# Scale and shift of the MLP's LayerNorm input: from whole rows on GpSimd ahead of the transposes to columns on ScalarE behind them

## The chip, the core and the metric

The kernel runs on one core of a Trainium2 chip. The metric is the device time of one execution in microseconds (us); of several runs the median is taken. The kernel before took 2519.69 us in the median of three runs (2519.55 to 2523.37).

A core has a matrix engine (PE, TensorE), whose weight loads the profile lists apart (PEld), and three engines that work on 128 partitions at a time: VectorE (DVE), ScalarE (ACT) and GpSimd (POOL). SyncE (SP) issues the loads and most stores. They work side by side, each in its own program order, and wait for one another by semaphores. Operands lie in SBUF; PE writes its products to PSUM, which DVE and ACT read.

## The reference, cut to what matters

One inference step of one decoder layer for a prompt of 2048 tokens and 32 sample tokens, in fp32, of width 1024:

```python
mixed = jnp.einsum('bte,ed->btd', jnp.concatenate([y_ssm, y_att], -1), w_out)
x = layer_norm(ALPHA * x + g_m * mixed, ln1_g, ln1_b)
h = x * (1.0 + sc_f) + sh_f
u = jnp.square(jax.nn.relu(jnp.einsum('btd,df->btf', h, w_up)))
f = jnp.einsum('btf,fd->btd', u, w_down)
x = layer_norm(ALPHA * x + g_f * f, ln2_g, ln2_b)
```

`sc_f`, `sh_f`, `g_m` and `g_f` are rows of 1024 numbers, computed from the sequence's vector `c`; for the prompt there is one of each, the same for all its tokens. The LayerNorm's own gain and shift (`ln1_g`, `ln1_b`) and the two rows behind it fold into one scale and one shift for each of the 1024 columns: with the normalised row u, h = u A2 + B2, where A2 = ln1_g (1 + sc_f) and B2 = ln1_b (1 + sc_f) + sh_f.

## The kernel before

The program has three large stages: the input projection with the mixers (to about 790 us of the span), the **output projection** with LayerNorm 1 (790 to 1009 us), and the **MLP** (to the end). The change lies in the second.

**Precision.** Each fp32 matmul operand is split into a high and a low part (`split`, L160: a rounding copy by ScalarE is the high part at L161, source minus high part is the low part at L162, by DVE unless another engine is named). A product is then three matmuls (`mm3`, L165 to L167): high times high, high times low, low times high.

**The output projection** runs over sixteen tiles of 128 tokens. The steps of a tile t are functions:

- `out_a(t)` (L1037) loads the tile's two halves of the mixers' output into one staging buffer, transposes one of them on PE (four transposes, L1047), and splits both. The low part of the loaded half is POOL's for tiles 1 to 3 and DVE's otherwise.
- `out_x(t)` (L1054) loads the tile's residual and scales it by two DVE operations over 128x1024 (L1057, L1058), which read and write SBUF alone.
- `out_mm(t)` (L1062) is the projection, 2 x 8 x 3 = 48 matmuls of 128x512.
- `out_u(t)` (L1073) multiplies the result out of PSUM by the gate row (L1079), adds the residual (L1080), takes the statistics (L1081, L1082, L172; the power -1/2 on POOL, L173), forms one column `nbo` on DVE (L1085), and normalises on ScalarE (L1086) with that column and `rs` as bias and scale. The result u is stored (L1087), as the second LayerNorm's residual.
- `out_h(t)` (L1090) is h = u A2 + B2, two operations over 128x1024 on POOL (L1095, L1096), on DVE in the last tile. A2 and B2 are rows that `out_rows` (L1029) has spread over all 128 partitions: four broadcast loads of 512 KB and three DVE operations. h has a single buffer, `ho`.
- `out_c(t)` (L1107) transposes h on PE, two sets of four 128x128 (L1118), and splits each set out of PSUM: ScalarE copies 128x512 to the high part, DVE subtracts for the low part. Tiles 0 to 7 land in `H2`, which stays in SBUF for the MLP's first half; there a tile's 1024 numbers lie in eight strips of 128 with gaps. Tiles 8 to 15 go to `h2_d` in DRAM.

The code calls them as `out_mm(t)`, `out_u(t)`, `out_h(t)`, `out_c(t - 1)`. The order on each engine is not the code's order: a scheduler in the compiler sorts the instructions of all engines by a model of their times, so that PE's transposes of one tile stand among the matmuls of a later one.

**The MLP** starts with `up`, which squares the up-projection by DVE (L1261) and takes a low part by POOL (L1262), with weights that are loaded, scaled by a row `gf` on DVE (L1137) and split by ScalarE and POOL; and with `acc_init`, which turns eight tiles of stored u into the second residual by two DVE operations each (L1231, L1232). The buffers of `A2`, `B2`, `ho`, `x1` and `u1` serve the MLP as well.

Of the kernel before, what the change touches and what calls it, by code (L numbers as in the profile page):

```python
# [23 lines left out]
NTILE = T // 128  # L24
# [47 lines left out]
def host_arrays(i):  # L72
    a = {}
    f = lambda n: np.asarray(i[n])
    a["consts"], a["dmask"] = host_consts()
    a["x"] = np.concatenate([f("x_prompt")[0], f("x_sample").reshape(ND, DM)], 0)
    c = np.concatenate([f("c_prompt"), f("c_sample")], 0)
    a["cT"] = c.T.reshape(8, 128, 9).transpose(1, 0, 2)
    wa = f("w_ada")[0].reshape(8, 128, 6144)
    wc = wa[:, :, :2048].reshape(2, 4, 128, 2, 8, 128)[:, :, :, ::-1].transpose(4, 0, 2, 1, 3, 5)  # L80
    a["w_ac"] = wc.reshape(8, 2, 128, 1024)
    a["w_ada"] = wa[:, :, 2048:].reshape(8, 128, 8, 512).transpose(2, 1, 0, 3)
    col = lambda v: v.reshape(-1, 128).T
# [14 lines left out]
    a["normw"] = f("ssm_norm_w")
    a["rows"] = np.stack([f("ln_in_g"), f("ln_in_b"), f("ln1_g")[0], f("ln1_b")[0], f("ln2_g")[0], f("ln2_b")[0]], 0)
    wo = f("w_out")[0]  # L100
    att = wo[512:].reshape(2, 4, 64, 1024)[:, HR].transpose(1, 0, 2, 3).reshape(4, 128, 1024)
    a["wo"] = np.concatenate([wo[:512].reshape(4, 128, 1024), att], 0)
    a["wu"] = f("w_up")[0].reshape(8, 128, 32, 128).transpose(2, 1, 0, 3)
    a["wd"] = f("w_down")[0].reshape(32, 128, 1024)
    a["h0"] = f("state_ssm")[0].reshape(8, 512, 128).transpose(0, 2, 1)
    ck, cv = f("cache_k")[0], f("cache_v")[0]
    a["ckT"] = ck.transpose(3, 2, 0, 1).reshape(64, 2, 1024)
    a["ck"] = ck.reshape(8, 128, 128)
    a["cv"] = cv.reshape(8, 128, 128)
    return {k: np.ascontiguousarray(v) for k, v in a.items()}  # L110
# [8 lines left out]
def body(tc, I, O):  # L119
    nc = tc.nc  # L120
    V, S, G, PE, D = nc.vector, nc.scalar, nc.gpsimd, nc.tensor, nc.sync
# [3 lines left out]
    def pool(name, **kw):  # L125
        return tc.alloc_tile_pool(name=name, bufs=1, reuse_waits="tile", **kw)
# [9 lines left out]
    def sc_tile():  # L136
        return ps.tile([128, 512], F32, tag="sc", name="sc", bufs=3)
# [3 lines left out]
    ada_d = tc.dram_tile([9, 6 * DM], F32, name="ada_d")  # L141
# [18 lines left out]
    def split(hi, lo, src, eng=None):  # L160
        S.activation(hi, src, AF.Copy)  # L161
        (eng or V).tensor_tensor(lo, src, hi.bitcast(F32), ALU.subtract)  # L162
# [19 lines left out]
    def bcast(t, src):  # L182
        D.dma_start(out=t, in_=src.partition_broadcast(t.shape[0]))
        return t
# [11 lines left out]
    ident = idt[:, 0:128]  # L196
# [431 lines left out]
    blk = {}  # L628
# [56 lines left out]
    n = len(seq)  # L685
# [66 lines left out]
    for i in range(n + 3):  # L752
# [3 lines left out]
        t = g(i)  # L756
# [216 lines left out]
    def prt(i, dt_=F32):  # L973
        return pr.tile([128, 1024], dt_, tag=f"p{i}", name=f"p{i}")
# [19 lines left out]
    first2 = {}  # L994

    def q2(nm, dt_=F32):
        return first2.pop(nm) if nm in first2 else pr2.tile([128, 1024], dt_, tag=nm, name=nm)
# [11 lines left out]
    def o_y():  # L1009
        i = ocnt["y"]  # L1010
        ocnt["y"] += 1
        if i < 2:
            r = hb2[i][:, 0], hb2[i][:, 1]
        elif i == 2 or i > 3 and i % 3 == 0:
            r = prt(5, F32R), prt(6, F32R)
        else:
            r = [p3.tile([128, 1024], F32R, tag="y" + c, name="y" + c, bufs=2) for c in "hl"]
        return [t.rearrange("p (k n) -> p k n", k=8) for t in r]

    ag, ab_ = prt(2), prt(3)  # L1020
    orow = {}

    def ada_row(r, j, P):
        if P == 128:
            return bcast(r, ada_d[0, 1024 * j:1024 * j + 1024])
        D.dma_start(out=r[:ND], in_=ada_d[1:9, 1024 * j:1024 * j + 1024].unsqueeze(1).to_broadcast([NB, NT_, 1024]))
        return r

    def out_rows(P):  # L1029
        A2, B2 = [ada_row(t, j, P) for t, j in ((q2("A2"), 4), (q2("B2"), 3))]  # L1030
        g1 = bcast(q2("ho"), I["rows"][2])
        b1 = bcast(p3.tile([128, 1024], F32, tag="yh", name="b1", bufs=2), I["rows"][3])
        V.scalar_tensor_tensor(b1[:P], A2[:P], 1.0, b1[:P], ALU.add, ALU.mult)
        V.tensor_tensor(B2[:P], B2[:P], b1[:P], ALU.add)
        V.scalar_tensor_tensor(A2[:P], A2[:P], 1.0, g1[:P], ALU.add, ALU.mult)
        return A2, B2

    def out_a(t):
        P = ptok(t)
# [14 lines left out]
    def out_x(t):  # L1054
        x = o_x(t)
        D.dma_start(out=x, in_=I["x"][128 * t:128 * t + 128])
        V.scalar_tensor_tensor(x, x, mean_all[:, t, 0:1], ag, ALU.subtract, ALU.mult)  # L1057
        V.scalar_tensor_tensor(x, x, mean_all[:, t, 1:2], ab_, ALU.mult, ALU.add)  # L1058
        blk["ox", t] = x

    def out_mm(t):
        yh, yl = blk.pop(("o", t))  # L1062
        blk["om", t] = mms = []
        for n in range(2):
            sl = slice(512 * n, 512 * n + 512)
            mm = sc_tile() if t == 1 else mm_tile()
            for k in range(8):
                mm3(mm, yh[:, k, :], yl[:, k, :], Wo[k][0][:, sl], Wo[k][1][:, sl], k == 0, k == 7)
            mms.append(mm)
# [17 lines left out]
        D.dma_start(out=xhat1_d[128 * t:128 * t + 128], in_=u)  # L1087
        blk["ou", t] = u

    def out_h(t):  # L1090
        A2, B2 = orow[0]
        u = blk.pop(("ou", t))
        h = q2("ho")
        eng = V if t == NTILE - 1 else G
        eng.tensor_tensor(h, u, A2, ALU.mult)  # L1095
        eng.tensor_tensor(h, h, B2, ALU.add)  # L1096
        blk["h2", t] = h

    def out_b_dec():
        yh, yl = blk.pop(("o", NTILE))  # L1100
        ud = o_x(1)
        for n in range(2):
            sl = slice(512 * n, 512 * n + 512)
            mm_dec(ud[:, sl], 512, lambda k: yh[:, k, :2 * ND], lambda k, l: Wo[k][l][:, sl])
        S.dma_start(out=ud_d, in_=ud[:2 * ND])

    def out_c(t):  # L1107
        h = blk.pop(("h2", t))
        if t < 8:
            sl = slice(128 * (t % 4), 128 * (t % 4) + 128)  # L1110
            oh, ol = H2[t // 4][0][:, :, sl], H2[t // 4][1][:, :, sl]
        else:
            oh, ol = o_y()
        for j in range(2):
            tr = sc_tile().rearrange("p (k n) -> p k n", k=4)
            for kk in range(4):
                k = 4 * j + kk
                PE.transpose(tr[:, kk, :], h[:, 128 * k:128 * k + 128], ident)  # L1118
            split(oh[:, 4 * j:4 * j + 4, :], ol[:, 4 * j:4 * j + 4, :], tr)
        if t >= 8:  # L1120
            D.dma_start(out=h2_d[t - 8][:, 0], in_=oh.bitcast(F32))
            D.dma_start(out=h2_d[t - 8][:, 1], in_=ol.bitcast(F32))
# [18 lines left out]
    def wu_pq():  # L1141
        return [pq.tile([128, 1024], F32R, tag="wu" + c, name="wu" + c) for c in "hl"]
# [16 lines left out]
    pk.release()  # L1159
    cs_.release()  # L1160
    pr2 = pool("pr2", side="right")
    first2.update({nm: pr2.tile([128, 1024], F32, tag=nm, name=nm) for nm in ("x1", "u1", "A2", "B2", "ho")})
    pq = pool("wu", side="right")
    ph = pool("h2", side="right")
    H2 = [[ph.tile([128, 8, 512], F32R, name=f"H2_{j}{i}") for i in range(2)] for j in range(2)]
    p3 = pool("out")
    out_a(2)
    out_x(2)
    out_a(3)
    out_x(1)  # L1170
    orow[0] = out_rows(128)
    for t in range(NTILE):
        if t > 2:
            out_a(t + 1)
        if 1 < t < NTILE - 1:
            out_x(t + 1)
        if t > 1:
            out_mm(t)
        if t > 0:
            out_u(t)  # L1180
        out_h(t)
        if t > 0:
# [209 lines left out]
    for half in range(2):  # L1392
# [24 lines left out]
        for fb in range(15):  # L1417
            f = 2 * fb
# [19 lines left out]
        for j in range(3):  # L1438
            for i in range(2):
                a = 352 * j  # L1440
                while a < 352 * (j + 1):
                    e = min((a // 128 + 1) * 128, 352 * (j + 1))
                    D.dma_start(out=H3[j][i][:, :, a - 352 * j:e - 352 * j].bitcast(F32),
                                in_=h2_d[a // 128][:, i, :, a % 128:a % 128 + e - a])
                    a = e
# [78 lines left out]
```

## Time and profile before

| | |
|---|---|
| median of 3 runs | 2519.69 us (2519.55 to 2523.37) |
| the profiled execution | 2522.31 us |
| its span, first to last instruction | 2520.5 us |
| granted TensorE clock, mean | 0.985 |
| busy: PE / DVE / POOL / ACT | 96 / 60 / 37 / 29 % of the span |
| slices 14 to 16 of 40 (63 us each, 819 to 1008 us), busy in tenths: PE | 9, 8, 8 |
| the same: DVE / POOL / ACT | 9, 8, 8 / 5, 4, 4 / 2, 2, 2 |

How to read what follows. Times are us from the start of the span, unless marked ns. A row of a timeline has the start, the duration, the engine, the line of the program, the operation, what it writes and reads, and the shape (partitions x elements); "x4" means four instructions in a row, and the bracket at the end tells how long the engine stood idle ahead of it and what ended that. A row of groups has the count, the busy time in all, the mean of one in ns, and the idle time ahead of the group's instructions with what ended it. A row of waits reads "engine, what it was to write, its line <- engine, what that wrote, its line: us in total, times, the longest". L161, L162 and L165 to L167 are helpers' lines; there the names tell which step it is: `yh` and `yl` (or `p`) are the high and low parts of the mixers' output, `H` and some `yh`, `yl` those of h, `mm` the projection's result, `sc` and `tr` PSUM of the transposes, `pg` the projection's weights. Buffer numbers are left out there.

### The profile page before, as it was taken

To read this page: it belongs to the slowest core of one execution; us is meant where nothing else is said; L and a number is where in the kernel's file an instruction comes from. 1 tells how busy PE (TensorE), PEld (TensorE's weight loads), DVE (VectorE), ACT (ScalarE), POOL (GpSimd) and SP (SyncE) were. 2 spreads that over 40 slices of the span, in tenths; PEclk is the share of its full clock that TensorE was granted. 3 is DMA by queue.
4 is the path that set the end of the run, shared out by engine and by line. 5 is a ranking of instruction groups with operands and counts; after the bars stand their busy time and mean duration, and the time that the engine had idled before them with its cause. 6 is when DMAs were issued, how large, how long until landed. Compare 5 with 4: busy or idle time off the path is not lost.

```text
span 2520.5 us, 32205 instructions
## 1 busy us (share of the span) xinstructions
PE 2421.1 (96%) x12694; PEld 2004.7 (80%) x12694; DVE 1510.5 (60%) x2582; ACT 720.2 (29%) x1434; POOL 930.8 (37%) x602
## 2 busy tenths in 40 slices
PE   7899999999998988899999999999999999999997
PEld 6567787977997766787888888887788988988985
DVE  6756666977788988744434444447844344344347
ACT  3544465333342222222121211213221221221221
POOL 4323431233223544633243333426532332332335
PEclk9999999999999999899999999999999999999998
DMA  8644333223335336411111211118211111111111
GB/s 318 255 173 160 118 124 91 73 72 109 98 115 174 117 127 221 162 59 58 48 59 42 63 51 39 53 43 238 100 51 34 43 59 34 43 59 34 43 46 70
DMA packets 116504, 244.19 MB, mean 97 GB/s; under 512 B 25984, under 2 KB 61248, under 8 KB 113200
## 3 DMA queue, kind: packets, MB, share of 16 engines
q1 hardware_dynamic: 111952, 232.15, 27.6%
q10 hardware_dynamic: 4400, 9.98, 1.1%
q8 instruction: 100, 1.64, 0.3%
q14 instruction: 52, 0.43, 0.1%
HBM read 187.74 MB, written 55.37 MB: 96 GB/s over the span
## 4 chain that ended last, share of the span: by engine, by line
PE 53%; DVE 3%; POOL 1%; issue 1%; DMA 0%; ACT 0%; SPq 0%; POOLq 0%; DVEq 0%; ACTq 0%
PE sc L165 10%; PE sc L167 10%; PE sc L166 10%; PE mm L165 5%; PE mm L167 5%; PE mm L166 5%; PE tr L165 2%; PE tr L167 2%; PE tr L166 2%; PE tr L1276 1%; DVE p L1231 1%; DVE nb L1300 0%; DVE p L1232 0%; POOL rs L173 0%; DVE p L1307 0%
## 5 line engine op out<-in xcount | busy, mean ns | idle before, releaser
L162 POOL TENSOR_TENSOR wdl<-st,wdh 128x1024 fp32r<-128x1024 f32 x63 | 164.1, 2605 | 531.4 <-ACT wdh L161 531.4
L1261 DVE TENSOR_TENSOR r<-r 128x320 f32<-128x320 f32 (+1 forms) x160 | 151.3, 946 | 299.0 <-ACT u L1257 101.6
L1288 DVE TENSOR_TENSOR p<-mm,p 128x512 f32<-128x512 f32 x298 | 202.7, 687 | 176.6 <-PE mm L167 176.6
L161 ACT ACTIVATE wdh<-st 128x1024 fp32r<-128x1024 f32 x63 | 66.8, 1061 | 628.4 <-PE mm L167 245.4
L165 PE MATMUL sc<-H,wvh 128*128 128x352 f32 (+1 forms) x640 | 227.1, 355 | 5.3 <-ACT r L1255 5.3
L167 PE MATMUL sc<-H,wvl 128*128 128x352 f32 (+1 forms) x640 | 226.1, 353 | 0.0
L166 PE MATMUL sc<-H,wvh 128*128 128x352 f32 (+1 forms) x640 | 225.9, 353 | 0.0
L165 PE MATMUL sc<-H,wuh 128*128 128x352 f32 (+1 forms) x640 | 224.4, 351 | 0.0
L167 PE MATMUL sc<-H,wul 128*128 128x352 f32 (+1 forms) x640 | 223.9, 350 | 0.0
L166 PE MATMUL sc<-H,wuh 128*128 128x352 f32 (+1 forms) x640 | 223.6, 349 | 0.0
L1255 ACT ACTIVATE r<-sc 128x352 f32<-128x352 f32 (+1 forms) x160 | 81.7, 511 | 271.6 <-PE sc L167 230.9
L165 PEld LDWEIGHTS sc<-H,wvh 128*128 128x128 f32 x640 | 120.8, 189 | 18.3 <-ACT r L1255 5.7
L166 PEld LDWEIGHTS sc<-H,wvh 128*128 128x128 f32 x640 | 120.7, 189 | 12.0
L167 PEld LDWEIGHTS sc<-H,wvl 128*128 128x128 f32 x640 | 120.4, 188 | 12.1
L165 PEld LDWEIGHTS sc<-H,wuh 128*128 128x128 f32 x640 | 120.4, 188 | 11.4 <-ACT r L1255 0.8
L167 PEld LDWEIGHTS sc<-H,wul 128*128 128x128 f32 x640 | 120.8, 189 | 10.5
L166 PEld LDWEIGHTS sc<-H,wuh 128*128 128x128 f32 x640 | 120.7, 189 | 10.2
L1137 DVE TENSOR_TENSOR st<-st,gf 128x1024 f32<-128x1024 f32 x64 | 83.8, 1309 | 55.6 <-POOL wdl L162 46.3
L1288 DVE TENSOR_TENSOR p<-tr,p 128x512 f32<-128x512 f32 x102 | 69.9, 687 | 74.8 <-PE tr L167 74.8
L173 POOL TENSOR_TENSOR rs<-ve,mhalf 128x1 f32<-128x1 f32 (+2 forms) x68 | 49.1, 722 | 174.9 <-DVE ve L172 158.1
L1260 DVE TENSOR_TENSOR ud<-r 128x32 f32<-128x32 f32 x32 | 56.5, 1766 | 94.4 <-ACT r L1255 94.4
L652 DVE SCALAR_TENSOR_TENSOR xc<-xq,cvw,xc 128x256 f32<-128x256 f32 x192 | 102.0, 535 | 2.7
(485 smaller groups left out, 6630.8 us busy)
## 6 DMA issues: line engine op xcount, KB each, us to landing
st<-in_wd SPq DMA_DIRECT2D x64, 512.0 KB
st<-in_wu SPq DMA_DIRECT2D x63, 512.0 KB
wa<-in_w_ada SPq DMA_DIRECT2D x32, 512.0 KB
hT_d<-hb SPq DMA_DIRECT2D x16, 1024.0 KB
hT<-hT_d SPq DMA_DIRECT2D x16, 512.0 KB
hT<-hT_d SPq DMA_DIRECT2D x8, 1024.0 KB
csb<-cs_d SPq DMA_DIRECT2D x16, 512.0 KB
p<-xhat_d SPq DMA_DIRECT2D x16, 512.0 KB
```

Of the source, the lines that this page charges most:

```text
L161: S.activation(hi, src, AF.Copy)
L162: (eng or V).tensor_tensor(lo, src, hi.bitcast(F32), ALU.subtract)
L165: PE.matmul(out, lhsT=ahi, rhs=bhi, start=first, stop=False)
L166: PE.matmul(out, lhsT=ahi, rhs=blo, start=False, stop=False)
L167: PE.matmul(out, lhsT=alo, rhs=bhi, start=False, stop=last)
L173: G.tensor_tensor(r[:P], v[:P], mhalf[:P, 0:n], ALU.pow)
L652: V.scalar_tensor_tensor(dst_, src(j), cvw[:, f, j:j + 1], dst_, ALU.mult, ALU.add)
L1137: V.tensor_tensor(st, raw, scale, ALU.mult)
L1255: S.activation(r[:, :n], mm[:, :n], AF.Relu)
L1260: V.tensor_tensor(ud, r[:, w:n], r[:, w:n], ALU.mult)
L1261: V.tensor_tensor(r[:, :w], r[:, :w], r[:, :w], ALU.mult)
L1288: V.tensor_tensor(acc[t][:, sl], mm, acc[t][:, sl], ALU.add)
```

## The change

The scale and shift move behind the transpose. In a transposed tile the 1024 columns lie on the partitions, eight groups of 128, so A2 and B2 become columns: one number per partition and group, sixteen columns in all (`AB2`).

- `out_rows` and its rows go; `out_cols` takes their place: the two rows from DRAM are loaded as a 16x128 block and turned by one PE transpose, the two LayerNorm rows come from the host as 128x16 (`lcol`), and three small DVE operations form `AB2`. Buffers `A2` and `B2` are no longer taken in this stage.
- `out_h` goes. `out_c` transposes u itself.
- Behind the transposes ScalarE makes eight passes of 128x128, each with one column of A2 as scale and one of B2 as bias, out of PSUM into `ho`.
- The whole h is split at once: ScalarE's copy of 128x1024, and the subtraction of 128x1024 on POOL (on DVE in the last tile), where there were two copies out of PSUM and two subtractions on DVE.

```diff
+    a["lcol"] = np.concatenate([col(f("ln1_g")[0]), col(f("ln1_b")[0])], 1)
...
-    def out_rows(P):
-        A2, B2 = [ada_row(t, j, P) for t, j in ((q2("A2"), 4), (q2("B2"), 3))]
-        g1 = bcast(q2("ho"), I["rows"][2])
-        b1 = bcast(p3.tile([128, 1024], F32, tag="yh", name="b1", bufs=2), I["rows"][3])
-        V.scalar_tensor_tensor(b1[:P], A2[:P], 1.0, b1[:P], ALU.add, ALU.mult)
-        V.tensor_tensor(B2[:P], B2[:P], b1[:P], ALU.add)
-        V.scalar_tensor_tensor(A2[:P], A2[:P], 1.0, g1[:P], ALU.add, ALU.mult)
-        return A2, B2
+    def out_cols():
+        AB2 = pr2.tile([128, 2, 8], F32, name="AB2")
+        t_ = p3.tile([128, 1024], F32, tag="yh", name="lc", bufs=2)
+        r16 = t_[:16, 0:128]
+        D.dma_start(out=r16, in_=ada_d[0, 3072:5120].rearrange("(k p) -> k p", p=128))
+        lc = t_[:, 128:144].rearrange("p (a k) -> p a k", a=2)
+        D.dma_start(out=lc.rearrange("p a k -> p (a k)"), in_=I["lcol"])
+        tr = sc_tile()
+        PE.transpose(tr[:, 0:16], r16, ident[:16, :16])
+        for i in range(2):
+            V.scalar_tensor_tensor(AB2[:, i], tr[:, 8:16], 1.0, lc[:, i], ALU.add, ALU.mult)
+        V.tensor_tensor(AB2[:, 1], AB2[:, 1], tr[:, 0:8], ALU.add)
+        return AB2
...
-    def out_h(t):
-        A2, B2 = orow[0]
-        u = blk.pop(("ou", t))
-        h = q2("ho")
-        eng = V if t == NTILE - 1 else G
-        eng.tensor_tensor(h, u, A2, ALU.mult)
-        eng.tensor_tensor(h, h, B2, ALU.add)
-        blk["h2", t] = h
...
     def out_c(t):
-        h = blk.pop(("h2", t))
+        u = blk.pop(("ou", t))
...
+        h = q2("ho").rearrange("p (k n) -> p k n", k=8)
         for j in range(2):
             tr = sc_tile().rearrange("p (k n) -> p k n", k=4)
             for kk in range(4):
                 k = 4 * j + kk
-                PE.transpose(tr[:, kk, :], h[:, 128 * k:128 * k + 128], ident)
-            split(oh[:, 4 * j:4 * j + 4, :], ol[:, 4 * j:4 * j + 4, :], tr)
+                PE.transpose(tr[:, kk, :], u[:, 128 * k:128 * k + 128], ident)
+            for kk in range(4):
+                k = 4 * j + kk
+                S.activation(h[:, k, :], tr[:, kk, :], AF.Identity, bias=AB2[:, 1, k:k + 1], scale=AB2[:, 0, k:k + 1])
+        split(oh, ol, h, V if t == NTILE - 1 else G)
```

The lines of the changed kernel are one to five higher: L1052 has the transposes of `out_a`, L1062 and L1063 the residual, L1084 to L1091 `out_u`, L1115 the transposes of u, L1118 the eight passes, L162 and L163 the split, L166 to L168 `mm3`.

The scheduler orders the changed program anew. On PE, the place is where the transposes of a middle tile stand. Before, those of tile 2's h (`ho_8410`) were in the midst of the 48 matmuls of tile 5 (`mm_8676`):

```order
L167 MATMUL mm_8676<-pg8_8027,yl_8534 128x512
L165 MATMUL mm_8676<-pg10_8031,yh_8533 128x512
L166 MATMUL mm_8676<-pg11_8032,yh_8533 128x512
L1118 MATMUL sc_8516<-idt_74,ho_8410 128x128 x4
L1118 MATMUL sc_8523<-idt_74,ho_8410 128x128 x4
L167 MATMUL mm_8676<-pg10_8031,yl_8534 128x512
L165 MATMUL mm_8676<-pg12_8035,yh_8533 128x512
```

In the changed program, those of tile 3's u (`u1_8498`) stand at the end of tile 4's matmuls (`mm_8580`); the transposes of `out_a` for tile 6 (`p4_8644`) and the first matmuls of tile 5 (`mm_8662`) follow them:

```order
L166 MATMUL mm_8580<-pg6_8023,yh_8433 128x512
L167 MATMUL mm_8580<-pg7_8024,yh_8433 128x512
L168 MATMUL mm_8580<-pg6_8023,yl_8434 128x512
L1115 MATMUL sc_8624<-idt_74,u1_8498 128x128 x4
L1115 MATMUL sc_8633<-idt_74,u1_8498 128x128 x4
L1052 MATMUL tr_8649<-idt_74,p4_8644 128x128 x4
L166 MATMUL mm_8662<-pg8_8027,yh_8540 128x512
L167 MATMUL mm_8662<-pg9_8028,yh_8540 128x512
```

So the transposes follow their tile's matmuls by one tile where they followed by two to three, and now stand between two tiles' matmuls.

On DVE, the place is the end of the statistics of tile 3. Before, `nbo` had an operation on the next residual (L1057) ahead of it, and the two subtractions of h's low part (`H2_01`) came behind:

```order
L162 TENSOR_TENSOR p6_8637<-p4_8633,p5_8636 128x512
L1082 BN_AGGR mvo_8496<-bst_8497 128x2
L172 TENSOR_SCALAR ve_8505<-mvo_8496 128x1
L1057 SCALAR_TENSOR_TENSOR x1_8544<-x1_8544,mean_all_73,p2_8079 128x1024
L1085 SCALAR_TENSOR_TENSOR nbo_8509<-mvo_8496,rs_8506 128x1
L1058 SCALAR_TENSOR_TENSOR x1_8544<-x1_8544,mean_all_73,p3_8080 128x1024
L162 TENSOR_TENSOR H2_01_8252<-sc_8413,H2_00_8251 128x4x128
L162 TENSOR_TENSOR H2_01_8252<-sc_8420,H2_00_8251 128x4x128
```

In the changed program `nbo` (L1090 there) comes right behind the statistics:

```order
L1087 BN_AGGR mvo_8499<-bst_8500 128x2
L173 TENSOR_SCALAR ve_8508<-mvo_8499 128x1
L1090 SCALAR_TENSOR_TENSOR nbo_8512<-mvo_8499,rs_8509 128x1
L163 TENSOR_TENSOR yl_8541<-tr_8542,yh_8540 128x512
L163 TENSOR_TENSOR p6_8648<-p4_8644,p5_8647 128x512
L1062 SCALAR_TENSOR_TENSOR x1_8551<-x1_8551,mean_all_73,p2_8079 128x1024
```

The residual's operations moved behind `nbo`, and the subtractions of h left DVE.

The third place is DVE at the start of the MLP. Before, two squares (L1261, the second is shown) stood ahead of the stream of L1231:

```order
L1137 TENSOR_TENSOR st2_9858<-st_9934,gf_9862 128x1024
L1261 TENSOR_TENSOR r_9925<-r_9925 128x512
L1231 TENSOR_TENSOR p2_9947<-p2_9947,ag1_9865 128x1024
L1231 TENSOR_TENSOR p3_9949<-p3_9949,ag1_9865 128x1024
L1231 TENSOR_TENSOR p7_9957<-p7_9957,ag1_9865 128x1024
L1231 TENSOR_TENSOR p4_9959<-p4_9959,ag1_9865 128x1024
L1231 TENSOR_TENSOR p1_9961<-p1_9961,ag1_9865 128x1024
L1137 TENSOR_TENSOR st2_9943<-st_9941,gf_9862 128x1024
```

In the changed program (L1260 and L1230 there) the second square comes behind the stream:

```order
L1137 TENSOR_TENSOR st2_9920<-st_9996,gf_9924 128x1024
L1230 TENSOR_TENSOR p2_10009<-p2_10009,ag1_9927 128x1024
L1230 TENSOR_TENSOR p3_10011<-p3_10011,ag1_9927 128x1024
L1230 TENSOR_TENSOR p7_10019<-p7_10019,ag1_9927 128x1024
L1230 TENSOR_TENSOR p4_10021<-p4_10021,ag1_9927 128x1024
L1230 TENSOR_TENSOR p1_10023<-p1_10023,ag1_9927 128x1024
L1230 TENSOR_TENSOR p0_10029<-p0_10029,ag1_9927 128x1024
L1137 TENSOR_TENSOR st2_10005<-st_10003,gf_9924 128x1024
L1260 TENSOR_TENSOR r_9987<-r_9987 128x512
```

So one square of the first up-projection moved from ahead of some seven operations of 128x1024 to behind them.

More of the change, by code (lines that the diff above doesn't have):

```diff
@@ L1020, in body @@
     ag, ab_ = prt(2), prt(3)
-    orow = {}
     def ada_row(r, j, P):
@@ L1161, in body @@
     pr2 = pool("pr2", side="right")
-    first2.update({nm: pr2.tile([128, 1024], F32, tag=nm, name=nm) for nm in ("x1", "u1", "A2", "B2", "ho")})
+    first2.update({nm: pr2.tile([128, 1024], F32, tag=nm, name=nm) for nm in ("x1", "u1", "ho")})
     pq = pool("wu", side="right")
@@ L1170, in body @@
     out_x(1)
-    orow[0] = out_rows(128)
+    AB2 = out_cols()
     for t in range(NTILE):
@@ L1180, in body @@
             out_u(t)
-        out_h(t)
         if t > 0:
```

## The prediction

> **What bounds the kernel now.** I read the page's busy times and its chain, then the stretches of the output projection, then what PE waits for there, then the timelines of PE, DVE and POOL around those waits.
>
> ```profile
> PE 2421.1 (96%) x12694; PEld 2004.7 (80%) x12694; DVE 1510.5 (60%) x2582; ACT 720.2 (29%) x1434; POOL 930.8 (37%) x602
> ...
> PE 53%; DVE 3%; POOL 1%; issue 1%; DMA 0%; ACT 0%; SPq 0%; POOLq 0%; DVEq 0%; ACTq 0%
> ```
>
> PE sets the end; so a change gains only where PE stands idle or runs at a lower clock. The edit lies in the output projection, whose stretches are (columns: length, busy PE, weight load, DVE, ACT, POOL, granted clock, DMA share and rate):
>
> ```profile
> 808.80:996.80 188.00, 167.17 (x789) 135.20 (x788) 163.28 (x199) 45.52 (x68) 87.19 (x43) 0.97 0.43 148
> 996.80:1009.30 12.50, 9.98 (x49) 6.54 (x48) 7.45 (x10) 3.84 (x6) 5.70 (x3) 0.94 0.75 251
> 1009.30:1060.00 50.70, 43.07 (x174) 34.37 (x173) 39.12 (x29) 16.90 (x23) 32.66 (x9) 0.88 0.54 182
> ```
>
> The first holds the matmuls of tiles 3 to 15: 188.0 / 13 = 14.46 us a tile. The second holds the sample rows and the last two sets of transposes, the third the start of the MLP. A tile without a wait looks like this:
>
> ```profile
> 906.66 0.60 PE L1047 MATMUL tr<-idt,p 128*128 128x128 f32 x4
> ...
> 912.37 1.03 PE L1118 MATMUL sc<-idt,ho 128*128 128x128 f32 x8
> ...
> 918.95 0.60 PE L1047 MATMUL tr<-idt,p 128*128 128x128 f32 x4
> ```
>
> From one L1047 set to the next are 12.29 us: 48 matmuls, eight transposes of h, four of L1047. Thirteen such tiles and the one set of eight beyond that falls in the stretch (0.8 us) make 160.6, so **27.4 us are lost** there. Of the 12.5 us behind it, 32 matmuls at about 0.23 and two sets of eight fill 9.1: another 3.4. Sum 30.8 us. PE's waits from 790 to 1060 (total, times, longest) say where:
>
> ```profile
> PE mm L167 <- DVE yl L162: 9.7, 2, 5.7
> PE sc L1118 <- POOL ho L1096: 8.0, 4, 2.8
> PE mm L166 <- POOL wdl L162: 3.9, 1, 3.9
> PE mm L167 <- POOL B L1262: 3.7, 1, 3.7
> PE mm L167 <- DVE p L162: 3.6, 1, 3.6
> PE sc L1118 <- DVE ho L1096: 2.5, 1, 2.5
> PE sc L1118 <- DVE H L162: 1.1, 2, 0.6
> ```
>
> 8.0 + 2.5 are waits for h itself, 1.1 for the split behind it. The 9.7 are waits for DVE, which was late because POOL's two operations hold it up:
>
> ```profile
> 832.20 2.41 POOL L1095 TENSOR_TENSOR ho<-p,A 128x1024 f32<-128x1024 f32 x1 [0.71 <-PE sc L1118]
> 834.68 3.26 POOL L1096 TENSOR_TENSOR ho<-ho,B 128x1024 f32<-128x1024 f32 x1
> ...
> 862.93 3.34 POOL L1096 TENSOR_TENSOR ho<-ho,B 128x1024 f32<-128x1024 f32 x1
> ...
> 832.41 3.27 DVE L1057 SCALAR_TENSOR_TENSOR x<-x,mean_all,p 128x1024 f32<-128x1024 f32 x1 [1.56 <-DMA x<-in_x]
> 835.61 2.35 DVE L1085 SCALAR_TENSOR_TENSOR nbo<-mvo,rs 128x1 f32<-128x1 f32 x1
> ...
> 864.71 0.69 DVE L162 TENSOR_TENSOR H<-sc,H 128x512 fp32r<-128x512 f32 x1 [0.65 <-ACT H L161]
> ```
>
> nbo, one column, takes 2.35 us and ends at 837.96, when POOL's operation ends (837.94); the H subtraction, which reads PSUM, runs through POOL's next one in its usual 0.69. So DVE operations on SBUF alone wait for POOL. Over the stage, the means of nine DVE groups against their undisturbed values (1.28 and 0.15 us for the first and the last) add up to some 44 us, 2.9 a tile:
>
> ```profile
> L1057 DVE SCALAR_TENSOR_TENSOR p<-p,mean_all,p 128x1024 f32<-128x1024 f32 x6 | 14.6, 2430 | 6.4 <-DMA p<-in_x 6.4
> ...
> L1085 DVE SCALAR_TENSOR_TENSOR nbo<-mvo,rs 128x1 f32<-128x1 f32 x15 | 11.1, 741 | 7.2 <-POOL rs L173 7.2
> ```
>
> **The change, part by part.**
>
> ```profile
> L1096 POOL TENSOR_TENSOR ho<-ho,B 128x1024 f32<-128x1024 f32 x15 | 45.8, 3055 | 1.1
> L1095 POOL TENSOR_TENSOR ho<-p,A 128x1024 f32<-128x1024 f32 x8 | 19.6, 2449 | 15.6 <-DVE A L1035 7.3 <-ACT p L1086 6.3 <-PE sc L1118 2.0
> ...
> L162 POOL TENSOR_TENSOR wul<-p,wuh 128x1024 fp32r<-128x1024 f32 x1 | 2.4, 2412 | 2.4 <-ACT wuh L161 2.4
> ...
> L162 DVE TENSOR_TENSOR H<-sc,H 128x512 fp32r<-128x512 f32 x16 | 10.6, 682 | 1.1 <-ACT H L161 1.1
> L1086 ACT ACTIVATE u<-u,nbo,rs 128x1024 f32<-128x1024 f32 x8 | 10.0, 1244 | 42.5 <-DVE nbo L1085 42.5
> ...
> L161 ACT ACTIVATE wuh<-p 128x1024 fp32r<-128x1024 f32 x1 | 1.1, 1062 | 3.2 <-DMA p<-in_wu 3.2
> ...
> L367 ACT ACTIVATE v<-mm 128x128 f32<-128x128 f32 x14 | 3.8, 272 | 0.0
> ```
>
> *POOL.* Out go 2.45 + 3.06 us a tile, in comes one subtraction of 128x1024: 2.41 by the wul row. For tiles 0 to 7 its output lies in strips of 128 with gaps, which no POOL row shows; bounds 2.41 and 3.34 (the longest above), value 2.6.
>
> *DVE.* Out go two subtractions of 0.68. It was busy 163.28 / 13 = 12.56 us a tile. Minus 14 x 2 x 0.68 / 13 = 1.46, and with the hold-up cut from 2.9 to 1.4 (in step with POOL's 5.5 to 2.6; at worst 3.3 us, all of it) it needs 9.6, at worst 11.5. Its idle time was (188.0 - 163.28) / 13 = 1.9 a tile. 11.5 is under PE's 12.29; the worst, 13.4, is over it.
>
> *ACT.* Per tile two copies of 0.59 become eight passes of 128x128 with column scale and bias and one copy of 1.06. A pass is 0.27 by the L367 row, and two column operands cost 1.24 - 1.06 = 0.18: 2.2 to 3.6 us for eight, value 3.0. That adds some 2.9 us to 3.5 busy a tile (45.52 / 13): 6.4 of 12.3, hidden by ACT's idle time; were ACT the path it would cost 13 x 2.9 = 38. [...]
>
> *PE.* The transposes read u, not h; they come at the end of the following tile's matmuls (the order shows it), one tile after u's matmuls instead of up to three. Their number stays; one of 16 columns is added (0.1 us). The 8.0, 2.5 and 1.1 go. What is late next is u: from the last L1079 of a tile to the end of ACT's u were 4.7 to 12.8 us before, and 12.25 are there now. The two longest had nbo behind an x load on DVE; now nbo stands ahead. Cost nothing; the price is in the rivals.
>
> *Rows and columns.* Four broadcasts of 512 KB and three DVE operations of 1.22 go, two small loads come. PE's wait of 3.6 at 796.69 is not freed: DVE still has an x load in front of that split, and PE has a further L1047 set ahead of it, whose load is issued at about 791 and takes 2.6 (812.90 to 815.54) to 4.9 us (789.87 to 794.75):
>
> ```profile
> 794.75 1.28 DVE L1057 SCALAR_TENSOR_TENSOR x<-x,mean_all,p 128x1024 f32<-128x1024 f32 x1 [2.23 <-DMA x<-in_x]
> ...
> 812.90 0.32 SPq L1042 DMA_DIRECT2D p<-yn_d  x1
> ...
> 815.54 0.63 PE L1047 MATMUL tr<-idt,p 128*128 128x128 f32 x4 [0.62 <-DMA p<-yn_d]
> ```
>
> So -3.6 to +1.5 there; I take 0.
>
> *Start of the MLP.* 3.9 + 3.7 are waits for POOL while DVE streams over SBUF:
>
> ```profile
> 1036.31 14.30 POOL L162 TENSOR_TENSOR wdl<-st,wdh 128x1024 fp32r<-128x1024 f32 x1 [3.39 <-ACT wdh L161]
> ...
> 1024.95 9.05 DVE L1231 TENSOR_TENSOR p<-p,ag 128x1024 f32<-128x1024 f32 x5
> ```
>
> The same work follows in a slightly other order: 0, with 7.6 gained at best and, with the second square behind the stream, some 8 lost.
>
> *Sum.* 30.8 us are lost now. I keep 4 of them (0.3 a tile for thirteen tiles, by DVE's margin of 0.8 us): 26.8 gained, 27 with rounding. The profiled execution took 2522.31 us, 1.8 more than its span; 2522.3 - 27 = 2495. It lies 2.6 above the median of the three runs, so against the median of 2519.69 I say **2493**.
>
> **Rivals.**
>
> *DVE stays the pace.* POOL's subtraction holds DVE for all its 3.3 us and DVE needs 13.4 a tile: 13 x (14.46 - 13.4) = 14, plus the 3.4 at the end: 2502 to 2506. For it: DVE at 163 of 188. Against it: its hold-up was only half of POOL's time. [...]
>
> *The wait moves to the start of the MLP.* The second square on DVE is late, POOL's low parts behind it too: 8 us back, 2501.
>
> *Slower: u comes late.* PE is in order, so the eight transposes of u now hold the next tile's matmuls. If u took L from the last L1079, every second tile would wait L - 12.25. Break-even is at (L - 12.25) / 2 x 13 = 27, L = 16.4. At 18 us, +10: 2530. For it: 12.8 once. Against: most were 5 to 9, and the longest had a cause that the order removes.
>
> **How the numbers follow.** Forecast 0.62 (2483 to 2499); DVE the pace 0.22; MLP start 0.09; u late 0.07. Below, everything lost comes back with the 7.6 at the MLP: 2482; above, the DVE rival with the MLP's 8: 2512. Within 0.2%, 5 us, nothing can be told from no change by such runs. Faster by more: 0.62 and nearly all of 0.31, less what falls short: 0.85; slower: 0.07; between: 0.08.
>
> **What would show it.** PE's waits of L1115 (the new transposes) for ACT near zero, and L1052 sets 12.3 us apart: right. nbo still at 2.4 us under one POOL subtraction with tiles at 13 or more: the DVE rival. Transposes waiting for L1091's u: the slower one. A gap over 8 us within 50 us of the MLP's first matmul: the MLP rival. Wrong altogether if the eight passes take 0.6 us each or the strided subtraction 5 us.

## The result, and the profile after

The changed kernel took **2483.89 us** (median of 4 runs, 2483.55 to 2485.34), the kernel before 2521.53 us beside it (4 runs, 2519.55 to 2524.80). The ratio is 0.9849, with a 95% interval of 0.9835 to 0.9864: 37.6 us less. The forecast was 2493, with a range of 2482 to 2512. The profiled execution took 2483.86 us, 38.5 less than that of before.

Where they went is seen from one place in the program, the first matmul of the MLP. It started at 1009.33 us before, and at 978.07 now: **31.3 us** were gained by then. From there to the end were 2520.5 - 1009.33 = 1511.2 us, and are now 2482.0 - 978.07 = 1503.9: another **7.2 us**, in a stage that the change does not name.

First the busy times of the page, then the output projection from its first full tile to the first matmul of the MLP, and the start of the MLP (columns as in the table by stretches above: length, busy PE, weight load, DVE, ACT, POOL, granted clock, DMA share and rate):

```profile
PE 2407.5 (97%) x12695; PEld 2000.0 (81%) x12695; DVE 1466.3 (59%) x2549; ACT 764.0 (31%) x1546; POOL 883.4 (36%) x587
...
809.20:978.07 168.87, 168.87 (x827) 139.08 (x825) 124.99 (x172) 85.51 (x169) 46.40 (x30) 1.00 0.51 179
...
978.07:1028.80 50.73, 43.38 (x178) 34.59 (x177) 40.40 (x29) 20.01 (x30) 32.20 (x10) 0.90 0.52 188
```

In the output projection PE is busy for all of its 168.87 us, at a granted clock of 1.00. Before, the same stage showed 0.97 and 0.94. Matmuls behind its longest wait ran slower as well: after the wait of 5.70 us that ended at 939.70 they came 0.43 us apart for some 3 us (granted clock 0.51 from 940 to 943 us), where 0.23 is usual. The loss that the prediction read from the lengths held both. PE's waits from 775 to 1050 us are all that is left:

```profile
PE mm L168 <- POOL B L1261: 4.2, 1, 4.2
PE mm L167 <- POOL wdl L163: 3.2, 1, 3.2
PE tr L1052 <- DMA p<-yn_d: 1.7, 1, 1.7
PE mm L166 <- ACT p L162: 0.7, 1, 0.7
PE mm L168 <- DVE p L163: 0.7, 1, 0.7
```

The first two lie in the MLP's start (for the same two tensors they were 3.7 and 3.9 us before), the other three ahead of tile 3. No transposes of u wait. A middle tile, on PE:

```profile
857.95 1.04 PE L1115 MATMUL sc<-idt,u 128*128 128x128 f32 x8
858.82 0.60 PE L1052 MATMUL tr<-idt,p 128*128 128x128 f32 x4
...
871.04 0.60 PE L1052 MATMUL tr<-idt,p 128*128 128x128 f32 x4
```

From one set to the next are 12.22 us, what 48 matmuls and 12 transposes take. The other engines in the tile ahead of it:

```profile
848.95 0.16 DVE L1090 SCALAR_TENSOR_TENSOR nbo<-mvo,rs 128x1 f32<-128x1 f32 x1 [0.72 <-POOL rs L174]
...
851.66 2.33 DVE L1062 SCALAR_TENSOR_TENSOR x<-x,mean_all,p 128x1024 f32<-128x1024 f32 x1 [1.45 <-DMA x<-in_x]
...
846.10 2.90 ACT L1118 ACTIVATE ho<-sc,AB 128x128 f32<-128x128 f32 x8 [5.46 <-PE sc L1115]
...
850.51 2.40 POOL L163 TENSOR_TENSOR H<-ho,H 128x1024 fp32r<-128x1024 f32 x1 [1.59 <-ACT H L162]
```

Eight passes on ScalarE take 2.90 us. POOL's subtraction takes 2.40. The eight tiles whose output lies in strips have a mean of 2.55, by the row of the group below, but only because one of them took 3.44; the middle value is 2.40 there too, so the strips cost nothing here:

```profile
L163 POOL TENSOR_TENSOR H<-ho,H 128x1024 fp32r<-128x1024 f32 x8 | 20.4, 2545 | 18.0 <-ACT H L162 18.0
```

In the tile above the subtraction holds one operation of DVE, L1062: 851.66 + 2.33 = 853.99, 1.08 us after POOL's end at 852.91, where it takes 1.28 alone. There nbo is through 1.4 us before POOL begins.

### The profile page after: what moved, and what is told of

The parts are those of the page before. It is cut to its first block, busy times and chain, and to the rows that moved or that the text cites. A ratio compares the mean times of both kernels' runs of the same rounds, so it can differ in the third digit from the quotient of the medians.

```text
span 2482.0 us, 32262 instructions
## 1 busy us (share of the span) xinstructions
PE 2407.5 (97%) x12695; PEld 2000.0 (81%) x12695; DVE 1466.3 (59%) x2549; ACT 764.0 (31%) x1546; POOL 883.4 (36%) x587
## 4 chain that ended last, share of the span: by engine, by line
PE 82%; DVE 10%; issue 3%; ACT 2%; POOL 2%; DMA 1%; POOLq 0%; DVEq 0%; SPq 0%; ACTq 0%
PE mm L166 12%; PE mm L168 12%; PE mm L167 12%; PE sc L166 11%; PE sc L167 11%; PE sc L168 11%; PE tr L166 2%; PE tr L168 2%; PE tr L167 2%; PE sc L462 1%; DVE xc L653 1%; PE mm L258 1%; DVE p L1230 1%; DVE csb L858 1%; PE tr L1275 1%
## 5 line engine op out<-in xcount | busy, mean ns | idle before, releaser
L163 POOL TENSOR_TENSOR wdl<-st,wdh 128x1024 fp32r<-128x1024 f32 x63 | 151.6, 2406 | 537.7 <-ACT wdh L162 537.6
L1260 DVE TENSOR_TENSOR r<-r 128x320 f32<-128x320 f32 (+1 forms) x160 | 146.4, 915 | 298.0 <-ACT u L1256 104.7
L162 ACT ACTIVATE wdh<-st 128x1024 fp32r<-128x1024 f32 x63 | 66.8, 1061 | 646.8 <-PE mm L168 263.3
L166 PE MATMUL sc<-H,wvh 128*128 128x352 f32 (+1 forms) x640 | 225.5, 352 | 5.5 <-ACT r L1254 5.5
L168 PE MATMUL sc<-H,wvl 128*128 128x352 f32 (+1 forms) x640 | 225.5, 352 | 0.0
L166 PE MATMUL sc<-H,wuh 128*128 128x352 f32 (+1 forms) x640 | 223.8, 350 | 0.0
L168 PE MATMUL sc<-H,wul 128*128 128x352 f32 (+1 forms) x640 | 223.1, 349 | 0.0
L166 PEld LDWEIGHTS sc<-H,wvh 128*128 128x128 f32 x640 | 120.6, 188 | 18.2 <-ACT r L1254 5.9
L168 PEld LDWEIGHTS sc<-H,wvl 128*128 128x128 f32 x640 | 120.5, 188 | 12.1
L166 PEld LDWEIGHTS sc<-H,wuh 128*128 128x128 f32 x640 | 120.1, 188 | 11.1 <-ACT r L1254 0.8
L168 PEld LDWEIGHTS sc<-H,wul 128*128 128x128 f32 x640 | 120.4, 188 | 10.3
L1261 POOL TENSOR_TENSOR ulx<-r,x 128x512 fp32r<-128x512 f32 (+2 forms) x52 | 76.6, 1475 | 83.5 <-DVE r L1260 83.5
```

The costliest lines, as they stand in the source:

```text
L166: PE.matmul(out, lhsT=ahi, rhs=bhi, start=first, stop=False)
L168: PE.matmul(out, lhsT=alo, rhs=bhi, start=False, stop=last)
L1260: V.tensor_tensor(r[:, :w], r[:, :w], r[:, :w], ALU.mult)
L1261: G.tensor_tensor(ul[:, o:o + w], r[:, :w], uh[:, o:o + w].bitcast(F32), ALU.subtract)
```

## The experiments

Two questions are open: which part of the change gave the 31.3 us, the wait for h or POOL's hold on DVE, and where the 7.2 us of the MLP come from. The times of before beside the runs were 2523.80, 2522.81, 2521.17 and 2524.67 us in the four sets.

### The wait for h, and the hold on DVE

**Without the two operations** (`b_noscale`), an edit of the kernel before, which leaves out the scale and shift:

```diff
-        h = q2("ho")
-        eng = V if t == NTILE - 1 else G
-        eng.tensor_tensor(h, u, A2, ALU.mult)
-        eng.tensor_tensor(h, h, B2, ALU.add)
-        blk["h2", t] = h
+        blk["h2", t] = u
```

> The kernel before with out_h left out (scale and shift are not applied, the transposes read u); the low parts are split on DVE out of PSUM as before. Theory 1 (the loss was POOL's two operations, by the wait for h and by holding DVE): the whole loss of the output projection goes, 27 to 31 us, about 2490 to 2494 with the buffers where they were. Theory 2 (DVE's own load was the pace, and the two subtractions that left it were part of the gain): 5 to 15 us of the loss stay, about 2500.

Measured: 2493.50 us (4 runs, 2492.80 to 2495.28), ratio 0.9883 (0.9870 to 0.9896). The MLP's first matmul stands at 979.38 us, and the stretch ahead of it reads like the changed kernel's, with DVE's two subtractions a tile still on DVE:

```profile
808.80:979.40 170.60, 170.60 (x835) 140.16 (x833) 123.87 (x206) 47.99 (x72) 12.11 (x15) 1.00 0.54 183
```

So theory 1 holds: the two operations (POOL's, and DVE's in the last tile) cost all of the 30 us. What DVE had to do of its own was not the pace. ScalarE's passes and POOL's subtraction give the scale and shift back without a loss. That the split left DVE isn't needed for the gain here; the changed kernel with its split still on DVE was not run.

**The operations beside the path** (`b_side`): they stay on POOL, but nothing reads their result, so the scale and shift are left out here as well.

```diff
-        blk["h2", t] = h
+        blk["h2", t] = u
```

> The kernel before with out_h's two POOL operations kept as they are, but the transposes read u: nobody reads their result (scale and shift do not reach the output). It parts the 30 us that leaving both operations out gave (2493.5 against 2523.8; first matmul of the MLP at 979.4 instead of 1009.3 us). If PE's wait for h made the loss: about 2494, the MLP starts near 980. If POOL's holding of DVE made it: about as before, 2515 to 2524, the MLP starts after 1000. Half and half gives 2508.

Measured: 2507.98 us (4 runs), ratio 0.9944 (0.9929 to 0.9959): half and half. The MLP's first matmul stands at 992.71 us. From 979.38 to there, 13.3 us are what POOL's operations cost by being there; from there to 1009.33, 16.6 us are what PE lost because h passed through them. (The scheduler orders some instructions anew when the dependence goes; by my estimate each half is good to a few us.) PE's waits, from 775 to 1080 us, show the turn:

```profile
PE mm L167 <- POOL B L1262: 9.6, 1, 9.6
PE sc L1118 <- ACT p L1086: 5.3, 2, 4.0
PE mm L167 <- DVE p L162: 3.1, 1, 3.1
PE sc L1118 <- ACT u L1086: 1.4, 1, 1.4
```

The first lies in the MLP's start. No wait names POOL's `ho` any more; the transposes wait for u. On DVE, L1058 of the residual shows the hold, first in `b_noscale`, then here (count, busy time and mean in ns):

```profile
L1058 DVE SCALAR_TENSOR_TENSOR x<-x,mean_all,p 128x1024 f32<-128x1024 f32 x8 | 10.3, 1281 | 0.0
...
L1058 DVE SCALAR_TENSOR_TENSOR x<-x,mean_all,p 128x1024 f32<-128x1024 f32 x8 | 15.3, 1914 | 0.0
```

nbo was caught in no tile of `b_side` (0.16 us each). Besides L1058, the hold lay on L1080, which adds the residual: the 16 such operations on u took 1.46 us in the mean, against 0.69 in `b_noscale`.

**The changed kernel with POOL filled again**, by one and by two operations that nothing reads (`a_pool1` has the first of the two below, `a_pool2` both):

```diff
         h = q2("ho").rearrange("p (k n) -> p k n", k=8)
+        if t < NTILE - 1:
+            z = q2("B2")
+            G.tensor_tensor(z, u, gm, ALU.mult)
+            G.tensor_tensor(z, z, gm, ALU.add)
```

> The changed kernel with one more operation of 128x1024 on POOL in tiles 0 to 14 (u times a row into a spare buffer, read by nothing): POOL has 2.4 + 2.65 + 0.5 = 5.6 us a tile, as much as before the change. With two, DVE worked without a gap at 15.4 us a tile, 6.4 of them held. If the hold grows with POOL's time, one less leaves 9.5 + 2 to 2.7 = 11.5 to 12.2 us a tile, just under PE's 12.25: 2484 to 2490. If the hold comes from the order (nbo caught behind POOL's subtraction), it comes back here as well: 2500 or more.

> The changed kernel with two more operations of 128x1024 on POOL in each of tiles 0 to 14 (u times a row into a spare buffer, that plus a row), whose result nothing reads: POOL is as full as before and more, but h does not pass through it. If the loss before was the wait for h alone: as the changed kernel, 2484. If POOL's holding of DVE made half of it: DVE needs 9.5 + 2.8 to 5.5 = 12.3 to 15 us a tile against PE's 12.25, so 1 to 36 us more; I expect +10 (2494), with nbo or the x operations at twice their time.

Measured: 2502.06 us with one (4 runs, 2499.91 to 2504.34; +18 against the changed kernel) and 2524.75 us with two (10 runs, 2523.34 to 2527.96; ratio to before 1.0008, 0.9999 to 1.0017). Two operations that nothing reads give back the whole gain, four times what I expected of them. How, shows DVE with one of them (the second pair is POOL):

```profile
855.24 2.34 DVE L1090 SCALAR_TENSOR_TENSOR nbo<-mvo,rs 128x1 f32<-128x1 f32 x1 [0.66 <-POOL rs L174]
...
859.41 3.29 DVE L1063 SCALAR_TENSOR_TENSOR x<-x,mean_all,p 128x1024 f32<-128x1024 f32 x1
...
868.48 2.33 DVE L1090 SCALAR_TENSOR_TENSOR nbo<-mvo,rs 128x1 f32<-128x1 f32 x1 [0.65 <-POOL rs L174]
...
855.17 2.40 POOL L163 TENSOR_TENSOR H<-ho,H 128x1024 fp32r<-128x1024 f32 x1
858.94 2.67 POOL L1113 TENSOR_TENSOR B<-u,p 128x1024 f32<-128x1024 f32 x1 [1.38 <-ACT u L1091]
```

POOL's subtraction now starts 0.07 us ahead of nbo, and nbo, which takes 0.16 alone, ends with it (857.58 and 857.57). The added operation catches L1063 (3.29 instead of 1.28). That makes 2.2 + 2.0 = 4.2 us of hold a tile; from nbo to nbo are 13.24 us, in which DVE has no gap but the 0.65 for `rs`. It has become the pace, 1.0 us over PE's 12.22. With two, the period in the middle tiles is 15.4. This is the prediction's DVE rival, brought about by added work. In these rows an operation on one column waits out the whole 2.40 us of POOL's.

So the hold was no fixed share of POOL's time: 4.2 us of 2.40 + 2.67 in this tile, some 1.2 of 2.40 a tile in the changed kernel. It went with which operation of DVE stood there when POOL began: nbo took 2.34 us here, and 0.16 in the changed kernel's tile above. On POOL the subtraction follows `rs`, and nbo waits for `rs` too. In these rows the subtraction has no idle time ahead of it: it starts as `rs` ends, and nbo is caught. In the changed kernel's tile above it still waited 1.59 us for ScalarE, and nbo got through. In three later tiles of that kernel it did not wait, and nbo took 2.34 or 2.35 us there as well (926.31, 938.53, 949.42), yet PE lost nothing. That in `a_pool1` one caught nbo makes the next tile's be caught, because u and all behind it come late, fits these rows but isn't shown.

### The pace of the MLP

Both kernels have PE busy without a gap from 1200 to 1600 us, at a granted clock of 1.00. Yet three pairs of up-projections with what lies between take 1389.57 - 1255.94 = 133.6 us before, and 1356.38 - 1223.38 = 133.0 now:

```profile
1255.94 0.39 PE L165 MATMUL sc<-H,wvh 128*128 128x512 f32 x1
...
1389.57 0.39 PE L165 MATMUL sc<-H,wvh 128*128 128x512 f32 x1
...
1223.38 0.40 PE L166 MATMUL sc<-H,wvh 128*128 128x512 f32 x1
...
1356.38 0.40 PE L166 MATMUL sc<-H,wvh 128*128 128x512 f32 x1
```

That is 44.54 and 44.33 us a pair, 192 matmuls each. The MLP holds some 33 such pairs: 7 us. One thing that differs is where buffers lie in SBUF: `AB2` takes 64 bytes per partition, so `x1`, `u1`, one more of these buffers, the up weights `wuh` and `wul` and the MLP's input `H2` lie 64 bytes lower, and `A2` and `ho` have changed places.

**Places exchanged between the kernels** (`b_layout`, `a_layout`): before with the places of the changed kernel, and the reverse, `AB2` then lying in the unused `A2`.

```diff
-    first2.update({nm: pr2.tile([128, 1024], F32, tag=nm, name=nm) for nm in ("x1", "u1", "A2", "B2", "ho")})
+    first2.update({nm: pr2.tile([128, 16 if nm == "pad" else 1024], F32, tag=nm, name=nm) for nm in ("x1", "u1", "ho", "pad", "B2", "A2")})
```

> The kernel before with nothing but the places of some SBUF buffers changed, to those of the changed kernel: a pad of 64 bytes, and A2 and ho in each other's place. Every engine has its instructions in the order of before. If the 7 us that the MLP became shorter by (1460.5 us from 1060.0 to the end before, 1453.2 from 1028.8 after) come from where the buffers lie, this kernel takes some 7 us less than before (about 2514) and the output projection stays at 188 us for its thirteen tiles. If they come from anything else (order, clock, other work beside it), it takes as long as before.

> The changed kernel with the buffers x1, u1, A2, B2, ho, the MLP's weights and H2 at the places that they had before. If place is what made the MLP faster: 7 us more than the changed kernel, about 2491, all of it behind the first matmuls of the MLP; the output projection as in the changed kernel (12.25 us a tile). If not: 2484.

Measured: `b_layout` 2516.72 us (11 runs; before 2523.80 in 22), ratio 0.9975 (0.9966 to 0.9983), 7.1 us less; `a_layout` 2491.32 us (4 runs), 7.4 more than the changed kernel. Each kernel takes the other's pace with the other's places: from the MLP's first matmul (1012.70 and 979.98 us, 3.4 and 1.9 later than with the kernel's own places) to the end are 1504.9 us in `b_layout` and 1512.0 in `a_layout`.

**Which of the two moves** (`a_pad`, `a_swap`, one run each): the 64 bytes alone, and the exchange of `A2` and `ho` alone, in the changed kernel.

> The changed kernel with A2 and ho in each other's place as before, but x1, u1, the third buffer, the MLP's up weights and H2 64 bytes lower as in the changed kernel. The distance from one pair of up-projections to the next in the MLP was 44.53 us with the old places and 44.32 with the new. If the 64 bytes do it: 44.32; if the exchange of A2 and ho does it: 44.53.

> The changed kernel with A2 and ho exchanged as in the changed kernel, but no buffer moved by 64 bytes. If the exchange makes the MLP faster: 44.32 us from one pair of up-projections to the next; if the 64 bytes do: 44.53.

Measured: 2484.02 and 2493.88 us; three pairs of up-projections take 132.9 us in `a_pad` and 133.6 in `a_swap`. The 64 bytes are the cause of the pace; the exchange does nothing for it.

**Other distances** (`a_top32`, `a_top96`, `a_top128`, one run each): a pad above all five buffers, which moves them down.

> The changed kernel with the old order of x1, u1, A2, B2, ho, and all five, the MLP's up weights and H2 moved down by 32 bytes. At 0 bytes the distance of two pairs of up-projections in the MLP was 44.53 us, with 64 bytes (A2 to ho not all moved) 44.27 to 44.32. If the pace falls steadily with the distance moved: about 44.4. If it hangs on the place within blocks of 64 bytes, 32 differs from both, either way. The output projection as in the changed kernel.

> The same with 96 bytes. If blocks of 64 bytes decide, as with 32 bytes; if blocks of 128 decide, the buffers' starts now stand in them as those of the down weights do, and the pace is its own: faster or slower than 44.3, I do not know which.

> The same with 128 bytes. If blocks of 128 bytes decide: 44.53 us again, as with 0 bytes, and some 2491 us for the whole. If blocks of 64 bytes decide: 44.53 as well, but then 64 bytes would not have changed anything. If only larger blocks decide: another pace.

Measured: 2487.02, **2467.07** and 2489.72 us. The stretch from 1200 to 1600 us has the same kind of work in all kernels; the count behind busy PE is that of the matmuls recorded in it. In order: before, `b_layout`, `a_layout`, `a_pad`, `a_top32`, `a_top96`, `a_top128`:

```profile
1200.00:1600.00 400.00, 400.00 (x1730) 323.90 (x1729) 172.66 (x200) 80.50 (x109) 141.38 (x72) 1.00 0.17 51
...
1200.00:1600.00 400.00, 400.00 (x1738) 324.85 (x1737) 174.47 (x203) 80.58 (x109) 141.32 (x72) 1.00 0.17 53
...
1200.00:1600.00 400.00, 400.00 (x1730) 323.77 (x1730) 171.29 (x199) 79.37 (x107) 141.25 (x72) 1.00 0.16 49
...
1200.00:1600.00 400.00, 400.00 (x1740) 324.97 (x1739) 171.61 (x199) 80.69 (x109) 141.63 (x73) 1.00 0.17 50
...
1200.00:1600.00 400.00, 400.00 (x1739) 325.09 (x1738) 172.22 (x200) 80.63 (x109) 141.22 (x72) 1.00 0.17 50
...
1200.00:1600.00 400.00, 400.00 (x1771) 331.16 (x1770) 177.46 (x205) 82.72 (x112) 144.50 (x74) 1.00 0.17 51
...
1200.00:1600.00 400.00, 400.00 (x1732) 323.72 (x1731) 171.24 (x199) 80.65 (x109) 141.05 (x72) 1.00 0.16 50
```

By the distance moved, with the place of `x1`, `wuh` and `H2` in blocks of 128 bytes as the program lays them out, and the mean time from one pair of up-projections to the next in the middle of the stage:

| moved by | start modulo 128 | pair of up-projections | per matmul |
|---|---|---|---|
| 0 (`a_layout`) | 96 | 44.54 us | 0.2320 us |
| 32 (`a_top32`) | 64 | 44.33 us | 0.2309 us |
| 64 (`a_pad`; `B2` and `ho` not moved) | 32 | 44.31 us | 0.2308 us |
| 96 (`a_top96`) | 0 | 43.52 us | 0.2267 us |
| 128 (`a_top128`) | 96 | 44.50 us | 0.2318 us |

The down weights, the other up weights (`wvh`, `wvl`) and `ulx` start at a multiple of 128 in every kernel. So at 96 all operands of the MLP's matmuls do, and the matmuls come 2.3% faster. At 128 the pace of 0 is back. In these runs the pace went with the place in blocks of 128 bytes (44.54 and 44.50 us at 96, 43.52 at 0). It did not go with the distance, and not with the place in blocks of 64, which is the same for 32 and 96 bytes (44.33 and 43.52).

The same traces tell more. The two up-projections of a pair do the same work on the same `H`, one with `wvh` and `wvl`, which never moved, the other with `wuh` and `wul`, which moved along with `H`. Here are the first matmuls of the one, of the other, of the down-projections behind them and of the next pair, in the changed kernel and in `a_top96`:

```profile
1223.38 0.40 PE L166 MATMUL sc<-H,wvh 128*128 128x512 f32 x1
...
1234.58 0.40 PE L166 MATMUL sc<-H,wuh 128*128 128x512 f32 x1
...
1245.49 0.40 PE L166 MATMUL mm<-wdh,u 128*128 128x512 f32 x1
...
1267.79 0.39 PE L166 MATMUL sc<-H,wvh 128*128 128x512 f32 x1
...
1222.12 0.39 PE L166 MATMUL sc<-H,wvh 128*128 128x512 f32 x1
...
1233.00 0.39 PE L166 MATMUL sc<-H,wuh 128*128 128x512 f32 x1
...
1243.88 0.39 PE L166 MATMUL mm<-wdh,u 128*128 128x512 f32 x1
...
1265.64 0.39 PE L166 MATMUL sc<-H,wvh 128*128 128x512 f32 x1
```

With `wvh` the 48 matmuls take 11.20 us in the changed kernel and 10.88 in `a_top96`, with `wuh` 10.91 and 10.88, and the 96 of the down-projections 22.30 and 21.76. In the kernel before and in `a_layout` the middle values are 11.21, 10.92 and 22.39. So the up-projection whose two operands lie alike in blocks of 128 was almost as fast at 96 or 32 modulo 128 as at 0: 10.92 and 10.91 us against 10.88. There, the 0.3 us of 11.2 went with one operand lying otherwise than the other, and 10.9 needed no multiple of 128. In the down-projections the operands were not parted: u lies in several buffers, and one of them, `ulx`, starts at a multiple of 128 as the weights do.

**A version that beats both** (`a_top96_wdl`): the 96 bytes, and the second open wait of the MLP's start.

```diff
-        return wtile("wd", f, t4("wdh"), t4("wdl"), gf)
+        return wtile("wd", f, t4("wdh"), t4("wdl"), gf, V if f < 2 else None)
```

> The changed kernel with the buffers moved by 96 bytes, as in the run of one look at 2467.07 us, and with the low parts of the first two down-projection weights (wdl) subtracted by DVE instead of POOL. Theory: behind the start of the MLP PE waits 3.0 us for the second wdl and 4.2 for a low part of u, because POOL stands still (one subtraction of 12.6 us) while DVE streams over SBUF; with wdl in DVE's own stream the 3.0 go, and some of the 4.2, as POOL has 2.4 us less to do: 2460 to 2464. Rival: the two subtractions lengthen DVE's stream, the low part of u comes later by as much as wdl comes earlier: 2467. The distance of two pairs of up-projections stays at 43.52 us in both cases.

Measured: **2459.23 us** (5 runs, 2457.93 to 2459.79; before 2524.67 in 9), ratio 0.9742 (0.9729 to 0.9756). PE's waits in the MLP's start were these with `a_top96`, and with this kernel the last row is all:

```profile
PE mm L168 <- POOL B L1261: 4.2, 1, 4.2
PE mm L167 <- POOL wdl L163: 3.0, 1, 3.0
...
PE mm L168 <- POOL B L1261: 3.6, 1, 3.6
```

The 3.0 are gone, and 0.6 of the 4.2: 3.6 us, about as expected; the whole time is 0.8 us below the expected range. The rest of the 7.8 against the one run of `a_top96` isn't accounted for by this stretch. The edit holds for the first two weights of the second half as well; from 1060 us to the end PE's waits on ScalarE and DVE sum to 7.0 us, against 9.4 in `a_top96`. What made that difference was not tried.

## Why the prediction was right, point by point

- **What bounded the kernel: right.** The loss was PE's, in this stage, 30.8 us by the prediction's count; 31.3 us came back by the MLP's first matmul. It is more than the count partly because a tile takes 12.22 us, not the 12.29 that the prediction took for one without a wait.
- **The waits for h: right,** 16.6 us of the gain by `b_side`. **POOL's hold on DVE: right as a mechanism,** 13.3 us by the same run. It was not all of the 9.7 us of waits for DVE: ahead of the two waits, L1057 and a subtraction took 5.35 and 5.27 us together, where 1.96 is usual, so the hold made some 6.7; DVE also stood 1.7 and 1.8 us there for a load of x. Nor did it reach every DVE operation on SBUF alone: before, a pass of the statistics (L1081, at 900.21) took its usual 0.68 us inside POOL's L1096 (899.13 to 901.92).
- **POOL's subtraction:** 2.40 us, in strips too, and 3.44 once; taken as 2.6. **ScalarE:** 2.90 us for eight passes, taken as 3.0. Hidden, as said: ScalarE is busy 85.5 of 168.9 us.
- **DVE's need:** right. Ten middle tiles, from 834.4 to 956.6 us, hold 96.1 us of DVE's work, 9.6 a tile; the prediction said 9.6. Of its hold of 1.4 us a tile, some 1.2 were found: nbo at a mean of 0.60 us instead of 0.15 (the three caught ones make it), the two x operations 10.5 us over their undisturbed 1.28 each. The rows:

```profile
L1062 DVE SCALAR_TENSOR_TENSOR p<-p,mean_all,p 128x1024 f32<-128x1024 f32 x6 | 14.1, 2351 | 6.8 <-DMA p<-in_x 6.7
...
L1090 DVE SCALAR_TENSOR_TENSOR nbo<-mvo,rs 128x1 f32<-128x1 f32 x15 | 8.9, 596 | 10.6 <-POOL rs L174 10.6
```

- **The reserve of 4 us for DVE's margin: too large.** Nothing of it was lost; tiles come at PE's own pace. This is the term that was mis-sized in the forecast stage.
- **u in time: right.** The last multiplication of a tile starts at 845.67, ACT's u ends at 851.56, and its transposes come at 857.95: 6 us to spare.
- **The start: right in size.** 3.6 + 0.7 us of waits became 1.7 + 0.7 + 0.7; the value taken was 0.
- **The start of the MLP: right.** 7.6 us of waits became 7.4.
- **The step that was missing: the pace of PE's matmuls in the MLP.** The sum had no term for it; "PE sets the end; so a change gains only where PE stands idle or runs at a lower clock" was wrong, since matmuls at a full clock and without a gap became 0.5% faster (44.54 to 44.33 us a pair of up-projections). 64 bytes of `AB2` did that, and `b_layout` and `a_layout` show it from both sides. With 31 + 7 the result came near the lower end of the range, by a way that the range was not made for: that it stayed inside is luck. With the buffers at their old places, `a_layout` took 2491.32 us, 2 from the forecast. (The lower end of 2482 is also not quite its own sum: 2519.69 - 30.8 - 7.6 is 2481.3.)
- **The DVE rival did not come, but by little.** `a_pool1` shows what it takes: one more operation on POOL a tile, no more POOL time than before the change, and DVE is the pace. The rival left 14 us of gain in the tiles for a DVE of 13.4 us each. That fits: in `a_pool1` nbo came every 13.36 us in the mean (829.46 to 963.08, ten tiles), and the MLP's first matmul stands at 994.85, 14.5 us earlier than before. In the changed kernel nbo is mostly out ahead of POOL's subtraction, and the three tiles that were caught in a row did not make DVE the pace.

## What to carry to other kernels

Here the operations on GpSimd cost 16.6 us on the path, and again 13.3 by what they held of VectorE (`b_side`). Before moving one, ask which VectorE operation will stand there when it begins: an operation on one column, once caught, took 2.34 us beside GpSimd's 2.40, where it takes 0.16 free (`a_pool1`). Where a change adds or drops even a small buffer, compare the matmul count of a gap-free stretch far from it, before and after: here buffers that moved by 64 bytes took a pair of up-projections, which the change never touches, from 44.54 to 44.33 us. Then try the places by themselves, with a pad, and look at where the two operands of a matmul lie relative to each other.

## What the runs showed of the hardware

- Matmuls of 128x512 in fp32 with all operands at multiples of 128 bytes came every 0.2267 us (10.88 for 48, `a_top96`). With both operands alike at 96 modulo 128 it was 10.92 for 48, or 0.2275 (the kernel before). With one at 0 and the other at 96 it was 11.21, or 0.2335, and with the other at 32 it was 11.18 (`a_layout`, changed kernel). Granted clock 1.00, PE busy without a gap in each. What in the chip does this, no run tells.
- VectorE's operation on one column took 0.16 us free, and 2.34 beside a GpSimd operation of 2.40 that had begun 0.07 us earlier (`a_pool1`).
- At the start of the MLP it was the reverse: one GpSimd subtraction of 128x512 took 12.60 us in `a_top96` while VectorE streamed over SBUF without a gap, against 1.29 for one at 800.77 us in the kernel before:

```profile
1005.41 5.75 DVE L1231 TENSOR_TENSOR p<-p,ab 128x1024 f32<-128x1024 f32 x5
...
1004.84 12.60 POOL L1261 TENSOR_TENSOR ulx<-r,x 128x512 fp32r<-128x512 f32 x1 [1.76 <-DVE r L1260]
```
